# Weight products that alternate between two accumulator banks

## The chip, the cores and the metric

The kernel runs on one core of one Trainium2 chip. The metric is the device time of one execution in microseconds (us). Three runs of the kernel before gave 1007.35, 1008.02 and 1010.14 us; the median is 1008.02. The engines are TensorE (PE, with its weight loads PEld apart), VectorE (DVE), ScalarE (ACT), GpSimd (POOL) and SyncE (SP, which issues the DMAs).

## The reference

Two layers of a hybrid block on 256 tokens of width 1024, all in float32. Cut to what matters:

```python
def hybrid_layer(x, ...):
    h = _rms(x) * norm1_g
    proj = h @ w_in                       # 1024 -> 7680 columns
    aq, ak, av, rw, rq, rk, rv, rg, gates = _split(proj, IN_SIZES)
    o_a = sliding_window_attention(_rms(aq), _rms(ak), av, sinks) @ w_attn_o
    o_b = rwkv7_time_mix(rw, ...) @ w_rwkv_o       # recurrence over the tokens
    o_c = retention(rq, rk, rv, rg) @ w_ret_o      # rotary, chunks of 128, decay
    g = jax.nn.sigmoid(gates)
    mixed = g[0] * o_a + g[1] * o_b + g[2] * o_c
    x = x + mixed @ w_out
    h2 = _rms(x) * norm2_g
    return x + (jax.nn.silu(h2 @ w_ffn_gate) * (h2 @ w_ffn_up)) @ w_ffn_down   # 1024 -> 2816 -> 1024
```

Every matrix product with a weight (`w_in`, the three branch outputs, `w_out`, the three of the FFN) streams its weight once through the core.

## The kernel before, in words

**Splitting.** A float32 product is made of three products in a faster 32-bit format: each operand is split into a high part (rounded) and a low part (what is left), and high x high, high x low and low x high are added up in one accumulator.

**Weight stream.** `wunit` fetches 128 partitions x 1024 weights by one DMA (tile `raw`), casts them on ACT to the high part `wh`, and subtracts on DVE to get the low part `wl`. Each of the three tiles has three buffers. There are 292 such units in the program. A unit 512 columns wide holds two k-tiles (k-tile: 128 rows of the contraction).

**Token-major products.** The 256 tokens are two blocks of 128, t = 0 and 1. `gemm_tok` (around line 517 of the kernel before) computes, for both blocks, an accumulator of 128 tokens x 512 columns, one PSUM bank each. The activations are the stationary operand (128x128: one k-tile, one block), the weights stream past. For a unit it runs the first block through, k-tile by k-tile with three products each (`mm3`: high x `wh`, high x `wl`, low x `wh`), six products into the first bank; then six for the second block into the second. The names of the accumulators are those in the traces: `rq`, `rk`, `rv`, `rg` (retention), `aq`, `akv` (attention), `gt` (gates), `po` (branch outputs), `px` (output projection), `pfg`, `pfu` (FFN gate and up), `pd` (FFN down).

**Channel-major products.** The RWKV columns (`pf`, around line 690) have the weights stationary and the 256 tokens streaming, two channel blocks f = 0, 1 with an accumulator each, four k-tiles a unit, 24 products 256 wide: f = 0 first, then f = 1.

**From one product to the next.** A result that feeds another weight product is transposed on TensorE and split again, block by block: transposes into a side bank (`ptn` after a norm, `ptm` after the mixing, `pto` for the RWKV output, `ptf` in the FFN, `pta` for the attention queries), a cast on ACT (`hth`, `mth`, `obh`, `ath`: the high part) and a subtraction on DVE (`htl`, `mtl`, `obl`, `atl`: the low part). The residual `x` is updated by DVE straight from the accumulators `px` and `pd`; `xg` is `x` times the norm's weight.

**PSUM.** Four banks are for the accumulators of the weight products (two GEMMs of two banks each), four for everything else.

**Order.** Nothing runs in the order in which it is written. Class `Program` records every instruction, plans an order for all engines at once with a list schedule of its own costs, and emits it at one line (L399 in every profile row). The products of the weight streams keep the order in which they were recorded; everything else on TensorE goes between them when the planner holds it ready. Readers of an accumulator and the DMAs, casts and subtractions of the units have priority rules of their own (`key`). So another order of the products also moves instructions on ACT and DVE. The waits are set afterwards from what each instruction reads and writes.

Of the kernel before, what the change touches and what calls it, by code (L numbers as in the profile page):

```python
# [84 lines left out]
class _Engine:  # L85
    """An engine whose calls are recorded."""

# [20 lines left out]
class Program:  # L108
    """Records the instructions, orders them for the engines and emits them in that order.

    The order is a list schedule: products of the weight streams keep their order and form the backbone of TensorE,
    everything else goes in between by the length of what hangs on it. Tile sets the waits; nothing here does.
    stream: instructions of one stream take the buffers of a pool in their order
    unit:   number of the weight tile that an instruction prepares (split) or multiplies (bulk)
    urgent: ahead of all else on its engine (what frees an accumulator, the first loads)
    """

# [148 lines left out]
    def forward(self, succ, need, bl):  # L266
# [35 lines left out]
        def blocked(i):  # L302
            """the tag whose slot the op lacks, or None; est is raised to the slots' release"""
            for t in ops[i]["touch"]:
                if t in placed:
                    continue
                k, q = kq = self.tiles[t]
                if not free[k]:
                    return k
                lst = self.tags[k][1][q]  # L310
                while nxt[kq] < len(lst) and lst[nxt[kq]] in placed:
                    nxt[kq] += 1
                if lst[nxt[kq]] != t:
                    return k
                f, a = min(free[k])
                if a:
                    est[i] = max(est[i], f + self.lat(a, ops[i]["eng"], True))
            return None
# [88 lines left out]
def hybrid_kernel(ctx: ExitStack, tc: tile.TileContext, A: dict, cst_d: bass.AP, out: bass.AP, layers=L):  # L407
# [88 lines left out]

# [1 line left out]
    wcount = [-1]  # L498
# [13 lines left out]
    def mm3(ps, xh, xl, wh, wl, first, last):  # L512
        mm(ps, xh, wh, first, False)
        mm(ps, xh, wl, False, False)
        mm(ps, xl, wh, False, last)

    def gemm_tok(w, lhs, nkt, n, ps, kt0=0, tot=None, tts=(0, 1)):
        """ps[t] += lhs(kt)[:, t]^T w ; w is [nkt*128, n] of the k-range starting at kt0 of tot."""
        tot = nkt if tot is None else tot
        nk = 1024 // n  # L520
        for u in range(0, nkt, nk):
            c = min(nk, nkt - u)
            wh, wl = wunit(w[u * 128:(u + c) * 128, :], c, n)
            for t in tts:
                for k in range(c):
                    kt = kt0 + u + k
                    xh, xl = lhs(kt, t)
                    rec.bulk = True
                    mm3(ps[t][:, :n], xh, xl, wh[:, k, :], wl[:, k, :], kt == 0, kt == tot - 1)
                    rec.bulk = False  # L530

# [10 lines left out]
    def split(pt, hi, lo):  # L542
        """pt PSUM [128, n, 128] -> hi/lo slices."""
        S.copy(hi, pt)
        tt(lo, pt, hi.bitcast(F32), SUB)

# [1 line left out]
    def new_norm():  # L548
# [30 lines left out]

    # first norm  # L580
    st = new_norm()
# [6 lines left out]

    # per-channel vectors of both layers, channel on the partitions
    vraw = ST([68, 128], "vraw")  # L590
# [28 lines left out]
    for l in range(layers):  # L619
# [4 lines left out]

        # per-layer small operands
        wa2 = TL(lp, [128, 512], F32, tag="wa2", name="wa2")
# [9 lines left out]

        # ---- retention query first: it needs the first norm tiles only in order --
        def rope(ps, t):
# [30 lines left out]

# [1 line left out]
        dg = TL(z_p, [128, 2, 128], F32, tag="hs", name="dg")  # L671
# [16 lines left out]
        for u in (6, 2, 3, 0, 1, 4, 5):  # L688
            pf = [PG([128, T], "pf") for _ in range(2)]
            for kg in range(2):  # L690
                wh, wl = wunit(w_in[kg * 512:(kg + 1) * 512, 768 + 256 * u:768 + 256 * (u + 1)], 4, 256)
                hh, hl = hts[kg]
                for f in range(2):
                    for k in range(4):
                        a, b = wh[:, k, f * 128:(f + 1) * 128], wl[:, k, f * 128:(f + 1) * 128]
                        fst, lst = (kg == 0 and k == 0), (kg == 1 and k == 3)
                        rec.bulk = True
                        mm(pf[f], a, hh[:, k, :], fst, False)
                        mm(pf[f], a, hl[:, k, :], False, False)
                        mm(pf[f], b, hh[:, k, :], False, lst)  # L700
                        rec.bulk = False
            rec.stream = 1
# [8 lines left out]
            if u == 6:  # L711
                act(wa[0:64, :], wa[0:64, :], AF.Tanh)
                act(sg, sg, AF.Tanh, scale=0.5)
                ts(sg, sg, 0.5, 0.5, MUL, ADD)
                # decay and in-context rate
                tw = RT([128, 4, T], "tw")
# [30 lines left out]
        def head_sums(src, name):  # L747
            """sums over the channels of every head: [token, token block, channel block, head of it]"""
            ph = PS([128, T], name)
            for p in range(4):  # L750
                mm(ph[32 * p:32 * p + 32, :], C("hsel"), src[:, p, :])
            hsm = TL(z_p, [128, T], F32, tag="hsm", name="hsm", bufs=1)
            S.copy(hsm, ph)
            pt = PS([128, 2, 4, 32], name + "t")
            for t in range(2):
                P.transpose(pt[:, t].rearrange("p a b -> p (a b)"), hsm[:, t * 128:(t + 1) * 128], ident)
            return pt[:, :, :, 0:2]

        def rwkv_rest():
            vcol = lambda nm, p: vec[:, vo[nm] + l * 4 + p:vo[nm] + l * 4 + p + 1]  # L760
            # removal key, its head norm
            kq = RT([128, 4, T], "kq")
# [41 lines left out]

            # within-chunk products; rows are the source token of b (own half) and k (other half)
            GA = RT([128, 4, 4, 64], "GA")
# [17 lines left out]

            # inverse of the unit triangular matrices: 32-blocks with a problem per partition
            Y = RT([128, 32, 32], "Y")
# [33 lines left out]

            # values, token-major, and stacked under the state of each chunk
            vt = RT([128, 2, 512], "vt")
# [11 lines left out]
            for par in range(2):  # L874
                G.memset(SV[0][HR[par], 0, :, par, :], 0.0)
            # bonus sums
            rk = RT([128, 4, T], "rk")
# [5 lines left out]

            # chunk recurrence
            ysb = [RT([128, 8, 64], "ysb") for _ in range(2)]
# [45 lines left out]

            # group norm, bonus, gate
            lnx = MT([128, 2, 512], "lnx")
# [39 lines left out]

# [1 line left out]
        rec.stream = 3  # L975
        psq = proj_tok(0, 512, "aq")
        psk = proj_tok(512, 256, "akv")
        # high parts of a head's rows, its low parts on the other half of the partitions
        qs = [TL(m_p, [128, 2, 4, 128], F32R, tag="m", name="aqs") for _ in range(2)]
# [46 lines left out]
        for t in range(2):  # L1026
            nk = 128 * (t + 1)
            am = C("amask")[:, 256 - nk:256]
            # head order here is (g, kv): head = 4*kv + g
            sc = [MT([128, 4, nk], "sc") for _ in range(2)]  # L1030
# [24 lines left out]
            for kvh in range(2):  # L1055
                for g in range(4):
                    h = kvh * 4 + g
                    act(sc[kvh][:, g, :], sc[kvh][:, g, :], AF.Copy, scale=dn[:, h:h + 1])
                for kc in range(t + 1):
                    pt = PS([128, 4, 128], "ptp")  # L1060
                    for g in range(4):
                        P.transpose(pt[:, g, :], sc[kvh][:, g, kc * 128:(kc + 1) * 128], ident)
                    # store in the order (kv, parity of the head, half)
                    o4 = pT[kc].rearrange("p (k b i) q -> p k i b q", k=2, b=2)
                    S.copy(o4[:, kvh], pt.rearrange("p (i b) q -> p i b q", b=2))
# [9 lines left out]

# [1 line left out]
        rec.stream = 2  # L1077
# [62 lines left out]

# [1 line left out]
        rec.stream = 4  # L1142
# [42 lines left out]
        rec.stream = 0  # L1185
# [1 line left out]
        gbc = load_g(A["norm2_g"], l)  # L1187
# [14 lines left out]

# [1 line left out]
        hT2 = lhs_of(st["tiles"])  # L1204
# [66 lines left out]
```

## Time and profile before

| what | before |
|---|---|
| runs, median (lowest to highest) | 1008.02 us (1007.35 to 1010.14) |
| span of the profiled execution | 1008.4 us, 14757 instructions |
| TensorE busy | 987.7 us, 98% of the span, 5749 products and transposes |
| its loads | 810.6 us, 80% |
| DVE busy | 698.5 us, 69% |
| ACT busy | 506.4 us, 50% |
| mean granted TensorE clock | 0.990 |
| weights and other data moved | 161.12 MB, 160 GB/s |

The profiled execution's span is 1008.4 us, 0.4 above the median of the runs. A row of a timeline gives the start in us, the duration, the engine, the line, the operation, what it writes and reads without the tiles' numbers, and how often; in square brackets stands the idle time before it and what ended that. Products on TensorE are pipelined, so the distance from one start to the next is what a product costs, not the duration in its row. In the chain of work that ended last a row joins consecutive pieces of one kind: start, length, engine, tile, count.

### The profile page before, as it was taken

The page shows a single profiled execution, that of the slowest core. Times are in us where ns is not written, and L with a number is a line of the kernel's source. Part 1 is how long each engine was busy: PE and PEld are TensorE (multiplying, and loading weights), DVE is VectorE, ACT ScalarE, POOL GpSimd, SP SyncE. Part 2 cuts the span into 40 slices and gives each one's busy share as a digit, 9 for nine tenths or more (in the row PEclk, how much of TensorE's full clock was granted, in tenths as well). Part 3 has the DMA queues.
Part 4 walks back from the last instruction along what each step waited for, and adds up shares of the span by engine and source line. Part 5 has one row for each costly group of instructions (what it writes and reads, how often), then busy time and mean ns, then how long its engine had stood idle before and what let it go on. Part 6 is the DMA issues. An engine that isn't in the chain of part 4 may idle for free.

```text
span 1008.4 us, 14757 instructions
## 1 busy us (share of the span) xinstructions
PE 987.7 (98%) x5749; PEld 810.6 (80%) x5749; DVE 698.5 (69%) x1056; ACT 506.4 (50%) x757; POOL 41.2 (4%) x32
## 2 busy tenths in 40 slices
PE   6999999999999999999999999999999999999998
PEld 5988777877778888898878887778777888888886
DVE  5759998995787555554476699899857665555544
ACT  5735466445455544443367345573544464444432
POOL 0010100000200000000000110001002000000000
PEclk9989999999999999999999799999999999999999
DMA  7535543443356666655544344434523565666553
GB/s 256 180 107 172 163 126 105 134 158 106 106 200 181 205 186 182 190 183 188 188 154 138 105 148 147 146 112 139 169 84 125 193 185 177 191 189 186 178 187 126
DMA packets 94352, 161.12 MB, mean 160 GB/s; under 512 B 5894, under 2 KB 26570, under 8 KB 94282
## 3 DMA queue, kind: packets, MB, share of 16 engines
q1 hardware_dynamic: 94282, 160.18, 50.3%
q8 instruction: 45, 0.74, 0.3%
q14 instruction: 25, 0.20, 0.1%
HBM read 159.11 MB, written 1.05 MB: 159 GB/s over the span
## 4 chain that ended last, share of the span: by engine, by line
PE 83%; DVE 12%; issue 2%; DMA 1%; POOL 1%; ACT 1%; SPq 0%; DVEq 0%; POOLq 0%
PE pd L399 12%; PE pfg L399 12%; PE pfu L399 12%; PE gt L399 10%; PE pf L399 8%; PE po L399 7%; PE px L399 4%; DVE wl L399 4%; PE rg L399 2%; PE rq L399 2%; DVE X L399 1%; PE py L399 1%; DVE BK L399 1%; PE pas L399 1%; PE ptf L399 1%
## 5 line engine op out<-in xcount | busy, mean ns | idle before, releaser
L399 DVE TENSOR_TENSOR wl<-raw,wh 128x1024 fp32r<-128x1024 f32 x292 | 356.7, 1222 | 217.2 <-ACT wh L399 216.2
L399 ACT CAST wh<-raw 128x1024 fp32r<-128x1024 f32 x292 | 306.8, 1051 | 345.4 <-PE pd L399 68.4
L399 PE MATMUL gt<-wh,hth 128*128 128x512 f32 x192 | 77.9, 406 | 0.0
L399 PE MATMUL gt<-wh,htl 128*128 128x512 f32 x192 | 77.4, 403 | 0.0
L399 PE MATMUL gt<-wl,hth 128*128 128x512 f32 x192 | 76.6, 399 | 0.0
L399 PE MATMUL pfg<-wl,hth 128*128 128x512 f32 (+1 forms) x192 | 72.5, 377 | 0.0
L399 PE MATMUL pfg<-wh,htl 128*128 128x512 f32 (+1 forms) x192 | 72.3, 376 | 0.0
L399 PE MATMUL pfg<-wh,hth 128*128 128x512 f32 (+1 forms) x192 | 71.6, 373 | 0.0
L399 PE MATMUL pfu<-wh,hth 128*128 128x512 f32 (+1 forms) x192 | 71.3, 371 | 0.0
L399 PE MATMUL pfu<-wl,hth 128*128 128x512 f32 (+1 forms) x192 | 71.3, 371 | 0.0
L399 PE MATMUL pfu<-wh,htl 128*128 128x512 f32 (+1 forms) x192 | 71.3, 371 | 0.0
L399 PE MATMUL pd<-wh,atl 128*128 128x512 f32 x176 | 69.4, 394 | 0.0
L399 PE MATMUL pd<-wl,ath 128*128 128x512 f32 x176 | 69.3, 394 | 0.0
L399 PE MATMUL pd<-wh,ath 128*128 128x512 f32 x176 | 69.3, 393 | 0.0
L399 PE MATMUL pf<-hth,wh 128*128 128x256 f32 x224 | 68.0, 304 | 0.0
L399 PE MATMUL pf<-hth,wl 128*128 128x256 f32 x224 | 67.1, 300 | 0.1
L399 PE MATMUL pf<-htl,wh 128*128 128x256 f32 x224 | 66.7, 298 | 0.0
L399 PEld LDWEIGHTS pf<-hth,wh 128*128 128x128 f32 x224 | 45.8, 204 | 6.6 <-issue 6.5
L399 PEld LDWEIGHTS pf<-hth,wl 128*128 128x128 f32 x224 | 45.9, 205 | 1.9 <-issue 1.6
L399 PEld LDWEIGHTS pf<-htl,wh 128*128 128x128 f32 x224 | 45.9, 205 | 1.7 <-issue 1.6
L399 PEld LDWEIGHTS gt<-wl,hth 128*128 128x128 f32 x192 | 36.1, 188 | 8.3 <-DVE wl L399 0.6
L399 PEld LDWEIGHTS gt<-wh,hth 128*128 128x128 f32 x192 | 36.1, 188 | 7.8 <-issue 0.5
(312 smaller groups left out, 1936.2 us busy)
## 6 DMA issues: line engine op xcount, KB each, us to landing
raw<-in_w_in_dram SPq DMA_DIRECT2D x120, 512.0 KB, 3.6
raw<-in_w_ffn_gate_dram SPq DMA_DIRECT2D x44, 512.0 KB, 3.5
raw<-in_w_ffn_up_dram SPq DMA_DIRECT2D x44, 512.0 KB, 3.5
raw<-in_w_ffn_down_dram SPq DMA_DIRECT2D x44, 512.0 KB, 3.6
raw<-in_w_out_dram SPq DMA_DIRECT2D x16, 512.0 KB, 3.9
raw<-in_w_attn_o_dram SPq DMA_DIRECT2D x8, 512.0 KB, 3.8
raw<-in_w_ret_o_dram SPq DMA_DIRECT2D x8, 512.0 KB, 3.5
raw<-in_w_rwkv_o_dram SPq DMA_DIRECT2D x8, 512.0 KB, 3.5
```

The costliest lines, as they stand in the source:

```text
L399: o["fn"](*o["args"], **o["kw"])
```

## The change

The products of a unit are recorded in another order. In `gemm_tok`, for each k-tile, the two token blocks alternate product by product, and so do the two banks; the three products of a block are now high x `wh`, low x `wh`, high x `wl`, so `wl` comes last rather than second. In the RWKV loop the two channel blocks alternate in the same way, for each k-tile. Number, shape and operands of the products, the loads and the DMAs are the same; the instruction that closes an accumulator is now a product with `wl`. The rest of the difference is comments and blank lines.

```diff
     def gemm_tok(w, lhs, nkt, n, ps, kt0=0, tot=None, tts=(0, 1)):
...
             wh, wl = wunit(w[u * 128:(u + c) * 128, :], c, n)
-            for t in tts:
-                for k in range(c):
-                    kt = kt0 + u + k
-                    xh, xl = lhs(kt, t)
-                    rec.bulk = True
-                    mm3(ps[t][:, :n], xh, xl, wh[:, k, :], wl[:, k, :], kt == 0, kt == tot - 1)
-                    rec.bulk = False
+            rec.bulk = True
+            for k in range(c):
+                kt = kt0 + u + k
+                xs = [lhs(kt, t) for t in tts]
+                fst, lst = kt == 0, kt == tot - 1
+                for i, t in enumerate(tts):
+                    mm(ps[t][:, :n], xs[i][0], wh[:, k, :], fst, False)
+                for i, t in enumerate(tts):
+                    mm(ps[t][:, :n], xs[i][1], wh[:, k, :], False, False)
+                for i, t in enumerate(tts):
+                    mm(ps[t][:, :n], xs[i][0], wl[:, k, :], False, lst)
+            rec.bulk = False
...
                 hh, hl = hts[kg]
-                for f in range(2):
-                    for k in range(4):
-                        a, b = wh[:, k, f * 128:(f + 1) * 128], wl[:, k, f * 128:(f + 1) * 128]
-                        fst, lst = (kg == 0 and k == 0), (kg == 1 and k == 3)
-                        rec.bulk = True
-                        mm(pf[f], a, hh[:, k, :], fst, False)
-                        mm(pf[f], a, hl[:, k, :], False, False)
-                        mm(pf[f], b, hh[:, k, :], False, lst)
-                        rec.bulk = False
+                rec.bulk = True
+                for k in range(4):
+                    fst, lst = (kg == 0 and k == 0), (kg == 1 and k == 3)
+                    for w, x, a, z in ((wh, hh, fst, False), (wh, hl, False, False), (wl, hh, False, lst)):
+                        for f in range(2):
+                            mm(pf[f], w[:, k, f * 128:(f + 1) * 128], x[:, k, :], a, z)
+                rec.bulk = False
```

What the planner makes of it is shown at three places. First TensorE at the border from the output projection to the FFN in layer one: the first products of `pfg_709` (t = 0) and `pfg_710` (t = 1), before:

```order
L399 MATMUL pfg_709<-wh_712,hth_683 128x512
L399 MATMUL pfg_709<-wl_713,hth_683 128x512
L399 MATMUL pfg_709<-wh_712,htl_684 128x512
L399 MATMUL pfg_709<-wh_712,hth_683 128x512
L399 MATMUL pfg_709<-wl_713,hth_683 128x512
L399 MATMUL pfg_709<-wh_712,htl_684 128x512
L399 MATMUL pfg_710<-wh_712,hth_683 128x512
L399 MATMUL pfg_710<-wl_713,hth_683 128x512
L399 MATMUL pfg_710<-wh_712,htl_684 128x512
```

Now, the same place:

```order
L399 MATMUL pfg_709<-wh_712,hth_683 128x512
L399 MATMUL pfg_710<-wh_712,hth_683 128x512
L399 MATMUL pfg_709<-wh_712,htl_684 128x512
L399 MATMUL pfg_710<-wh_712,htl_684 128x512
L399 MATMUL pfg_709<-wl_713,hth_683 128x512
L399 MATMUL pfg_710<-wl_713,hth_683 128x512
```

The first product with `htl` for the second block was the ninth and is the fourth. On DVE its last part, `htl_684<-ptn_689`, stands behind both updates of `x` from `px` in both orders.

Second, ACT at the border from the gates to the RWKV branch's output product (`po_635`, `po_636`): casts of the transposed RWKV output (`obh_337`, from the transposes `pto_345` for t = 0 and `pto_352` for t = 1), gate activations `tg` and casts of weight units, before:

```order
L399 CAST obh_337<-pto_345 128x4x128
L399 ACTIVATE tg_633<-gt_619,nhrs_126 128x512
L399 CAST obh_337<-pto_352 128x4x128
L399 ACTIVATE tg_634<-gt_620,nhrs_126 128x512
L399 CAST wh_650<-raw_649 128x1024
```

Now:

```order
L399 CAST obh_337<-pto_345 128x4x128
L399 CAST wh_650<-raw_649 128x1024
L399 ACTIVATE tg_633<-gt_619,nhrs_126 128x512
L399 ACTIVATE tg_634<-gt_620,nhrs_126 128x512
L399 CAST obh_337<-pto_352 128x4x128
```

The second cast of `obh` went behind a weight cast and both activations. On TensorE the transposes `pto_352` moved from the middle of the last gate unit to its end, right ahead of the first `po` product:

```order
L399 MATMUL gt_619<-wl_632,hth_116 128x512
L399 MATMUL gt_620<-wl_632,hth_116 128x512
L399 MATMUL pto_352<-cst_105,ysb_304 128x128 x4
L399 MATMUL po_635<-wh_638,obh_337 128x512
L399 MATMUL po_636<-wh_638,obh_337 128x512
L399 MATMUL po_635<-wh_638,obl_338 128x512
L399 MATMUL po_636<-wh_638,obl_338 128x512
```

Before, five products of `gt_620` came after `pto_352`, and then six of `po_635`; the first product of `po_636` was the seventh and is now the second.

Third, TensorE in the retention value product (`rv`), where the attention queries are transposed (`pta`), before:

```order
L399 MATMUL rv_454<-wl_463,hth_116 128x512
L399 MATMUL rv_454<-wh_462,htl_117 128x512
L399 MATMUL rv_454<-wh_462,hth_116 128x512
L399 MATMUL pta_386<-cst_105,qn_385 128x128 x4
L399 MATMUL ptk_387<-cst_105,kv_380 128x128
L399 MATMUL pta_395<-cst_105,qn_394 128x128 x4
L399 MATMUL ptk_396<-cst_105,kv_389 128x128
L399 MATMUL rv_454<-wl_463,hth_116 128x512
```

Now:

```order
L399 MATMUL rv_453<-wh_459,htl_109 128x512
L399 MATMUL rv_454<-wh_459,htl_109 128x512
L399 MATMUL rv_453<-wl_460,hth_108 128x512
L399 MATMUL pta_386<-cst_105,qn_385 128x128 x4
L399 MATMUL ptk_387<-cst_105,kv_380 128x128
L399 MATMUL pta_395<-cst_105,qn_394 128x128 x4
L399 MATMUL ptk_396<-cst_105,kv_389 128x128
L399 MATMUL rv_454<-wl_460,hth_108 128x512
```

`pta` moved up by one unit less one product: eleven products. On DVE the tile `GR`, whose operations free the side banks that `pta` takes, moved ahead of one weight subtraction (`wl_466`).

## The prediction

> **What bounds the kernel now.** I read the page first (busy shares, granted clock, chain that ended last), then TensorE's list of waits, then timelines of TensorE, VectorE (DVE) and ScalarE (ACT) wherever a product of a weight stream waits or nearly waits.
>
> ```profile
> PE 987.7 (98%) x5749; PEld 810.6 (80%) x5749; DVE 698.5 (69%) x1056; ACT 506.4 (50%) x757; POOL 41.2 (4%) x32
> ...
> PEclk9989999999999999999999799999999999999999
> ...
> PE 83%; DVE 12%; issue 2%; DMA 1%; POOL 1%; ACT 1%; SPq 0%; DVEq 0%; POOLq 0%
> ```
>
> TensorE is busy for 98% of the span at a clock of nine tenths or more, and the chain that ended last is mostly TensorE. So two things can move the time: the spacing of the products, and the places where TensorE stands still. The second are few (total us, times, longest):
>
> ```profile
> PE ptn L399 <- DVE xg L399: 6.7, 2, 6.5
> PE pta L399 <- DVE GR L399: 2.0, 2, 1.0
> PE pz L399 <- DVE Tn L399: 1.9, 2, 1.1
> PE pss L399 <- ACT kq L399: 1.2, 1, 1.2
> ...
> PE pto L399 <- DVE ysb L399: 1.1, 2, 0.6
> ```
>
> Apart from 6.7 us at the start they come to some 7 us. The spacing stands in the chain in order of time, and product by product in TensorE's timeline:
>
> ```profile
> 330.94 10.88 PE pfu L399 x48
> ```
> ```profile
> 376.14 0.39 PE L399 MATMUL pfu<-wh,hth 128*128 128x512 f32 x1
> ...
> 377.27 0.39 PE L399 MATMUL pfu<-wh,htl 128*128 128x512 f32 x1
> 377.50 0.39 PE L399 MATMUL pfu<-wh,hth 128*128 128x512 f32 x1
> 377.72 0.39 PE L399 MATMUL pfu<-wl,hth 128*128 128x512 f32 x1
> ```
>
> 10.88 us over 48 is 226.7 ns a product. 376.14 is the first pfu product of a unit, so 377.27 (five steps on) is the sixth and 377.50 the first into the other bank: 0.23 across the switch, 0.22 behind it.
>
> **Spacing: 0.** The change removes no product and no load. It makes a bank switch of every step where it was one in six, and the switch above costs what any other step costs. 3024 of the 3984 weight products are 512 wide, so 1 ns each would be 3 us. The one stage with another spacing is the down projection:
>
> ```profile
> 446.29 58.73 PE pd L399 x254
> ```
>
> That is 231.2 ns, 4.5 more than pfu; over its 528 products 2.4 us, and about as much again in po. [...] I take 0, with bounds of -4 (the excess gone) and +4 (doubled).
>
> **What moves: when the second token block's low part is needed.** Within a unit of two k-tiles the first block had six products before the second began, so the second block's low part was read by the ninth product. Now it is read by the fourth: five products, 5 x 0.227 = 1.13 us, earlier. And the two accumulators of a GEMM now end one product apart, so the first one's reader on DVE starts five products later than it could. Where one GEMM feeds the next, both squeeze the same DVE queue. I price each border by its rows.
>
> *px to pfg (output projection to FFN), each layer:*
>
> ```profile
> 319.31 0.39 PE L399 MATMUL pfg<-wh,hth 128*128 128x512 f32 x1
> ...
> 320.45 0.40 PE L399 MATMUL pfg<-wh,htl 128*128 128x512 f32 x1
> ```
> ```profile
> 318.35 1.28 DVE L399 SCALAR_TENSOR_TENSOR x<-px,x 128x512 f32<-128x512 f32 x2
> 319.55 0.68 DVE L399 TENSOR_TENSOR htl<-ptn,hth 128x512 fp32r<-128x512 f32 x1
> ...
> 1004.64 0.69 DVE L399 TENSOR_TENSOR x<-pd,x 128x512 f32<-128x512 f32 x1 [0.69 <-PE pd L399]
> ```
> ```profile
> 1004.21 0.39 PE L399 MATMUL pd<-wh,atl 128*128 128x512 f32 x1
> ```
>
> Before, htl was ready at 320.23 and read at 320.45. A reader that waits for an accumulator starts 0.43 us after its last product (1004.21 to 1004.64). 319.31 is pfg's fourth product, so px's last two stand four and five steps ahead of it, at 318.40 and 318.18. Now they close one bank each, so the reads begin at 318.61 instead of 318.35, and htl, behind both, is ready at 320.49. The fourth product would start at 319.31: a wait of 1.2 us, 2.4 for two layers. Below: 0.5 each, if ACT and DVE reach the reads idle and htl's transposes land between them.
>
> *po to px, each layer:*
>
> ```profile
> 295.46 0.39 PE L399 MATMUL px<-wh,mth 128*128 128x512 f32 x1
> ...
> 296.62 0.39 PE L399 MATMUL px<-wh,mtl 128*128 128x512 f32 x1
> ```
> ```profile
> 294.40 1.28 DVE L399 SCALAR_TENSOR_TENSOR tg<-tg,po 128x512 f32<-128x512 f32 x2
> 295.60 0.68 DVE L399 TENSOR_TENSOR mtl<-ptm,mth 128x512 fp32r<-128x512 f32 x1
> ```
>
> The same: 295.46 is px's fourth product, po's last but one, which now closes the first bank, stands five steps ahead of it at 294.30, its read at 294.73 instead of 294.40, mtl ready near 296.6, the fourth product due at 295.46: 1.15 each, 2.3 together (0.5 to 1.3 each).
>
> *gt to po of the RWKV branch, each layer.* Here the planner also moved four transposes (pto) from the middle of the last gate unit to its end, just ahead of po, and on ACT put a weight cast and two gate activations ahead of the cast obh that follows them.
>
> ```profile
> 281.19 0.69 ACT L399 ACTIVATE tg<-gt,nhrs 128x512 f32<-128x512 f32 x1 [0.34 <-PE gt L399]
> 281.86 0.59 ACT L399 CAST obh<-pto 128x512 fp32r<-128x512 f32 x1
> ...
> 283.61 1.04 ACT L399 CAST wh<-raw 128x1024 fp32r<-128x1024 f32 x1
> ```
> ```profile
> 281.97 1.28 DVE L399 TENSOR_TENSOR obl<-pto,obh 128x512 fp32r<-128x512 f32 x2
> ```
> ```profile
> 282.82 0.40 PE L399 MATMUL po<-wh,obh 128*128 128x512 f32 x1
> ```
>
> Before, both obl were done at 283.25. Now the cast that goes ahead needs the buffer of the last gate unit, free near 282.0; with 1.04 for it, twice 0.65 for the activations and 0.6 for obh, obh's second half is there at 284.9, obl's at 285.6. po's second product, the first of block 1, was due at 283.05: it waits 1.85, the fourth 0.2 more. I take 2.0 each, 4.0 together. Below: 0.8, if the ACT queue were empty (transposes end near 283.2, plus 0.6 for the cast). Above: 2.2.
>
> *pd to rq, the layer border, once:*
>
> ```profile
> 509.36 0.50 PE L399 MATMUL rq<-wh,htl 128*128 128x512 f32 x1 [1.14 <-DVE htl L399]
> ...
> 514.48 0.67 PE L399 MATMUL prb<-dg,cst 128*128 128x256 f32 x2 [0.83 <-DVE nhrs L399]
> ```
>
> By the new DVE order prb can start at 513.4, but with 10 products of rq behind it, not 17: 7 x 0.227 - 1.05 = +0.5 (0 to 1.5).
>
> *The end:* the two last additions come after both banks close, so the second runs behind the first: 0.43 + 0.6 after the product ahead of the last, +0.4.
>
> **Gains and the middle of a layer.**
>
> ```profile
> 10.69 0.68 DVE L399 TENSOR_TENSOR htl<-ptn,hth 128x512 fp32r<-128x512 f32 x1
> ```
> ```profile
> 10.83 0.80 PE L399 MATMUL rq<-wl,hth 128*128 128x512 f32 x1 [0.46 <-DVE wl L399]
> ...
> 11.85 0.63 PE L399 MATMUL rq<-wh,hth 128*128 128x512 f32 x1
> ```
>
> At the start the second product no longer needs wl, and the fourth can go when htl is there (11.4) instead of at 11.85: -0.25 (-0.43 to 0).
>
> ```profile
> 118.82 1.23 DVE L399 TENSOR_TENSOR wl<-raw,wh 128x1024 fp32r<-128x1024 f32 x1
> ```
> ```profile
> 120.64 0.63 PE L399 MATMUL pta<-cst,qn 128*128 128x128 f32 x4 [0.99 <-DVE GR L399]
> ```
>
> The attention transposes pta stand 11 products (2.5 us) earlier in TensorE's order, while only one weight subtraction (1.23) went behind GR on DVE: they wait 1.27 longer. DVE, though, is nearly full through this stretch:
>
> ```profile
> 100.00:125.00 25.00, 23.75 (x126) 19.64 (x126) 24.44 (x45) 11.42 (x19) 3.42 (x2) 1.00 0.53 162
> ```
>
> (window and its length, then the busy time of TensorE, its loads, DVE, ACT and GpSimd). It has the same work in the end, and pz, back at its old place but one product, waits 1.05 for it in the old order. A TensorE that is 1.27 late finds pz's operand there: 0.3 a layer, 0.6 together (each from -1.05, wait gone and nothing lost, to +1.3, nothing absorbed). The wait of pss in layer two falls by most of its 1.2, since about 12 narrow products now stand ahead of it: -0.9. pto's waits lose half: -0.6, the recurrence ahead of them having moved up three products. Last, the new order goes twelve times more from weight products to transposes and back. In the chain four transposes take, to what follows them,
>
> ```profile
> 121.38 0.44 PE pta L399 x4
> ...
> 128.58 0.59 PE ptb L399 x4
> ```
>
> so the place is worth at most 0.15: twelve by 0 to 0.15; at 0.05 each, since 0.44 is the commoner row, +0.6.
>
> **Sum:** -0.25 + 2.4 + 2.3 + 4.0 + 0.5 + 0.4 + 0.6 - 0.9 - 0.6 + 0.6 = +9.05 us on a profiled span of 1008.4, so 1017.4. The runs' median of 1008.02 lies 0.4 under that span; I forecast 1017.
>
> **Rivals.**
>
> *Faster: banks set the spacing.* If writing one bank back to back cost something, alternation would take it off every product. At 0.22, the smallest step in the rows above, it is 6.7 ns x 3024 = 20 us, less the 9 of the stalls: 997. It decides from 3 ns a product on. Against it: the switch row. [...]
>
> *No change: the queues give it back.* DVE's waits behind ACT are short and TensorE's six waits above shrink by whatever it is late. If px, po and pd lose half of their terms (4.8 instead of 9.6 with the end), pta and pz together give 2.1, pss and pto 2.3, and the excess in pd falls away (2.4), the span is 1008.4 + 4.8 - 6.8 = 1006.4, and with the excess kept 1008.8. For it: those waits exist. Against: the large terms stand at borders where TensorE waits for nothing today, so nothing is there to shrink.
>
> *Slower still: the middle isn't absorbed.* If pta's 1.3 stays and the softmax transposes, moved up by 22 products, lose up to 1.5 as well, each layer loses 2.5 more: 1022.4. It decides if DVE loses time to TensorE between 120 and 226 us.
>
> *The clock.* A step of rq in the first, cold microseconds is 0.43 (11.85, with 11.42 the product ahead of it), not 0.227. If alternation made the clock drop for a tenth of the span, the work of that tenth would take nearly twice as long: some 90 us more, 1098. The clock row shows nothing of the kind at today's switches. [...] Here no idle is seen at a switch.
>
> That the change does not take place can be left out: in the new order every pair of products alternates.
>
> **Chances.** Forecast (1011 to 1021) 0.62; not absorbed 0.13; no change 0.16; faster by spacing 0.06; clock 0.03. A measurement of this kernel tells about 0.3%, 3 us, from no change. Slower: 0.62 + 0.13 + 0.03 less a little of the forecast's low edge = 0.77. Same: 0.15. Faster: 0.06 and a third of what no change has below 1005 = 0.08. The range of 8 in 10 is 1009 to 1024: spacing bounds and the border terms' low ends below, the unabsorbed case above. The forecast's own range is 1011 to 1021.
>
> **What would show it.** Right: dense pfu still 10.9 us for 48; new entries in TensorE's waits of about 1.2 us for htl at pfg and mtl at px, about 2 us for obh and obl at po, twice each; pz's and pss's waits smaller; the end 0.4 later. Wrong: a changed pfu spacing (rival one), a clock row with low digits, border waits under 0.5, or pta's longer wait without a shorter one at pz.

## The result, and the profile after

The changed kernel took 1023.32 us (median of four runs, 1021.24 to 1025.01) against 1008.9 us for the kernel before (now the median of four): a ratio of 1.0134, 95% interval 1.0109 to 1.0160. It is slower by 14.4 us. I forecast slower, 1017, with 1009 to 1024 as the range: the direction held, the size was too small by 6 us, and it came partly from other places than I had said. That the time still lies inside the range, 0.7 us under its top, is luck in part, as the stretches below show.

The page of the changed kernel, busy times and granted clock:

```profile
PE 993.9 (97%) x5749; PEld 809.4 (79%) x5749; DVE 700.1 (68%) x1056; ACT 501.5 (49%) x757; POOL 38.6 (4%) x32
...
PEclk9999999999999999999999799999999999999999
```

The work is the same, and so is the mean clock (0.991, before 0.990); the span is 1023.2 instead of 1008.4. The dense stretches did not change either. TensorE's timeline in the FFN (pairs of products into the two banks):

```profile
340.03 0.62 PE L399 MATMUL pfu<-wl,hth 128*128 128x512 f32 x2
340.48 0.62 PE L399 MATMUL pfu<-wh,hth 128*128 128x512 f32 x2
340.94 0.61 PE L399 MATMUL pfu<-wh,htl 128*128 128x512 f32 x2
341.39 0.62 PE L399 MATMUL pfu<-wl,hth 128*128 128x512 f32 x2
```

1.36 us over six products is 227 ns, a bank switch at every step. So the loss is in waits. TensorE's list (total, times, longest) leads, behind the 5.9 us at the start, with four lines that the list before did not have:

```profile
PE po L399 <- ACT obh L399: 3.3, 2, 1.6
PE rk L399 <- ACT kv L399: 2.2, 2, 1.2
PE pfg L399 <- DVE htl L399: 2.1, 2, 1.1
PE px L399 <- DVE mtl L399: 2.1, 2, 1.1
PE pz L399 <- DVE Tn L399: 1.6, 2, 0.9
PE pta L399 <- DVE GR L399: 1.6, 2, 0.8
...
PE pto L399 <- DVE ysb L399: 0.7, 1, 0.7
PE pss L399 <- ACT kq L399: 0.7, 1, 0.7
```

Both kernels run the same products of the weight streams, unit by unit. So the start of a unit's first product in the changed kernel, less that in the kernel before, says how late the change has made the program by then (taken where both have as many transposes and other small products behind them). Its steps are where the time went:

| stretch | layer one | layer two | I had said, both layers |
|---|---|---|---|
| start (layer one) | -0.4 | | -0.25 |
| the border pd to rq | | +0.5 | +0.5 |
| rq and the RWKV columns (pf) | -2.3 | -0.8 | -0.9 |
| to the end of rk | +2.0 | +2.0 | nothing |
| rv, attention, first branch output | +2.2 | +2.2 | +0.6 with pz |
| to the last gate unit | -0.5 | -0.5 | nothing |
| gt to po (RWKV branch) | +3.9 | +1.4 | +4.0, and -0.6 for pto |
| po to px | +1.1 | +1.1 | +2.3 |
| px to pfg | +1.0 | +1.0 | +2.4 |
| rest of the FFN | +0.1 | +0.4 | 0 (spacing, -4 to +4) |
| the last additions | | +0.5 | +0.4 |

Apart from rounding they add up to 14.8, the difference of the two spans (the column of what I had said leaves out the 0.6 for changes between products and transposes, which has no stretch of its own). Each figure compares one execution with one execution, and the first rows depend on which: f1, g1 and g2 below have the changed kernel's order on TensorE, ACT and DVE well beyond the columns of layer one, and they reached the first product of aq 0.7 late, 2.9 early and 0.4 late; the changed kernel was 2.7 early. So neither the start's -0.4 nor the columns' -2.3 can be put down to the order.

**The two low-part borders** went as the prediction's working had it, here px to pfg in layer one, TensorE and then DVE:

```profile
325.06 0.39 PE L399 MATMUL pfg<-wh,htl 128*128 128x512 f32 x1
326.52 0.50 PE L399 MATMUL pfg<-wh,htl 128*128 128x512 f32 x1 [1.07 <-DVE htl L399]
```
```profile
324.58 1.29 DVE L399 SCALAR_TENSOR_TENSOR x<-px,x 128x512 f32<-128x512 f32 x2 [0.62 <-PE px L399]
325.79 0.68 DVE L399 TENSOR_TENSOR htl<-ptn,hth 128x512 fp32r<-128x512 f32 x1
```

DVE now waits for px to close (0.62), reads both banks, and only then makes the htl that the fourth product needs; 1.07 of TensorE's time passes.

**gt to po**, TensorE and ACT, layer one:

```profile
283.88 0.47 PE L399 MATMUL po<-wh,obh 128*128 128x512 f32 x1
286.00 0.50 PE L399 MATMUL po<-wh,obh 128*128 128x512 f32 x1 [1.64 <-ACT obh L399]
```
```profile
283.26 1.05 ACT L399 CAST wh<-raw 128x1024 fp32r<-128x1024 f32 x1 [1.26 <-PE gt L399]
284.21 1.26 ACT L399 ACTIVATE tg<-gt,nhrs 128x512 f32<-128x512 f32 x2
285.36 0.58 ACT L399 CAST obh<-pto 128x512 fp32r<-128x512 f32 x1
```

The queue on ACT is the one worked out: weight cast, two activations, then obh, and po's second product waits 1.64 for it.

**rk**, which I had not seen. TensorE and ACT, layer one:

```profile
94.58 0.39 PE L399 MATMUL rk<-wh,hth 128*128 128x512 f32 x1
96.16 0.50 PE L399 MATMUL rk<-wh,hth 128*128 128x512 f32 x1 [1.19 <-ACT kv L399]
```
```profile
94.69 1.05 ACT L399 CAST wh<-raw 128x1024 fp32r<-128x1024 f32 x1 [1.86 <-PE akv L399]
95.64 0.83 ACT L399 ACTIVATE kv<-akv,nrs 128x256 f32<-128x256 f32 x2
```

It is the second product of rk that waits, the first into its second bank, and what it waits for is not an operand: kv is the reading of akv, which frees a bank. In the old order the second bank was opened by the seventh product, and akv's first bank was closed and read while its second was still being filled. TensorE and ACT before, the first and the seventh product of rk and the two readings of akv:

```profile
97.29 0.40 PE L399 MATMUL rk<-wh,hth 128*128 128x512 f32 x1
...
98.68 0.39 PE L399 MATMUL rk<-wh,hth 128*128 128x512 f32 x1
```
```profile
96.05 0.47 ACT L399 ACTIVATE kv<-akv,nrs 128x256 f32<-128x256 f32 x1 [0.17 <-PE akv L399]
...
97.49 0.47 ACT L399 ACTIVATE kv<-akv,nrs 128x256 f32<-128x256 f32 x1 [0.62 <-PE akv L399]
```

One bank was read out at 96.52, before rk began, the other at 97.96, before rk's seventh product.

### The profile page after: what moved, and what is told of

It is laid out like the page before. It is cut to its first block, busy times and chain, and to the rows that moved or that the text cites. A ratio compares the mean times of both kernels' runs of the same rounds, so it can differ in the third digit from the quotient of the medians.

```text
span 1023.2 us, 14767 instructions
## 1 busy us (share of the span) xinstructions
PE 993.9 (97%) x5749; PEld 809.4 (79%) x5749; DVE 700.1 (68%) x1056; ACT 501.5 (49%) x757; POOL 38.6 (4%) x32
## 5 line engine op out<-in xcount | busy, mean ns | idle before, releaser
L399 PE MATMUL gt<-wh,hth 128*128 128x512 f32 x192 | 63.0, 402 | 0.0
L399 PE MATMUL pfg<-wh,htl 128*128 128x512 f32 (+1 forms) x192 | 57.0, 375 | 2.1 <-DVE htl L399 2.1
L399 PE MATMUL pfu<-wh,hth 128*128 128x512 f32 (+1 forms) x192 | 55.7, 371 | 0.0
L399 PE MATMUL pfu<-wl,hth 128*128 128x512 f32 (+1 forms) x192 | 55.7, 371 | 0.0
L399 PE MATMUL pfu<-wh,htl 128*128 128x512 f32 (+1 forms) x192 | 55.7, 371 | 0.0
L399 PE MATMUL pf<-htl,wh 128*128 128x256 f32 x224 | 49.5, 298 | 0.0
L399 PE MATMUL pf<-hth,wh 128*128 128x256 f32 x224 | 48.0, 297 | 0.0
L399 PE MATMUL pf<-hth,wl 128*128 128x256 f32 x224 | 47.4, 294 | 0.0
L399 PEld LDWEIGHTS gt<-wh,htl 128*128 128x128 f32 x192 | 35.3, 188 | 8.9 <-issue 1.2
L399 PEld LDWEIGHTS pfg<-wh,htl 128*128 128x128 f32 x192 | 35.0, 188 | 9.1 <-DVE htl L399 3.0
```

The source lines that it names most:

```text
L399: o["fn"](*o["args"], **o["kw"])
```

## Experiments

The theory after this reading: alternation is free in a dense stream; it costs at a few units where a GEMM meets the one ahead of it, because (a) the second block's operand is needed five products earlier, (b) two banks are opened at once and closed at once. The rival: something in alternating, or in the order of the three products, costs everywhere. Every ratio below is to the kernel before, measured in the same set of runs.

### Where in the stream it costs

**e1_pf_only**: only the RWKV loop alternates.

```diff
-            (gemm_tok as changed)
+            for t in tts:
+                for k in range(c):
+                    mm3(ps[t][:, :n], xh, xl, wh[:, k, :], wl[:, k, :], kt == 0, kt == tot - 1)
```

> Only the channel-major RWKV loop (pf) alternates between its two banks; every gemm_tok product is in the old order. Border theory (the loss comes from token block 1's low part being needed by the fourth instead of the ninth product, and from both accumulators of a token-major GEMM closing together): pf has no such border, its operands are ready for both channel blocks, so 1006 to 1011, no change. Rival (each alternating product costs something, about 14.4 us over 3984 products): pf is 960 narrow products, so +1.7 to +3.5 us, 1011 to 1012.

1009.49 us, ratio 0.9995 (0.9982 to 1.0007). No change: 672 alternating products cost nothing (pf has 672; the 960 of the expectation are all the narrow ones, and for 672 its rival gives at most 2.4 us).

**e2_inner_only** and **e3_edges_only** divide gemm_tok's units; pf is in the old order in both. The counts in the expectations are of the 126 units a layer that are 512 wide; six narrower ones are all edges.

```diff
+            if kt0 + u == 0 or kt0 + u + c == tot:    # e2: old order here; e3: old order elsewhere
+                (first block, then second, mm3)
+            else:
                 (alternating)
```

> gemm_tok alternates in every unit except the first and the last of a GEMM's contraction, which keep the old order; pf keeps the old order. That is 64 of 126 units a layer. Border theory: neither border is touched, 1007 to 1012, and no waits of pfg for htl, px for mtl or po for obh. Rival, a cost per alternating product: half of the loss, 1015 to 1017.

> The opposite: only the first and the last unit of a GEMM's contraction alternate, 62 of 126 units a layer; the units between and pf keep the old order. Border theory: nearly the whole loss, 1018 to 1024, with the waits of pfg for htl (1.0 each), px for mtl (1.1 each) and po for obh (1.6 each) as in the changed kernel. Rival, a cost per alternating product: half of the loss, 1015 to 1017, and half of these waits would be unexplained.

e2: 1009.22, ratio 0.9989 (0.9975 to 1.0003). e3: 1024.32, ratio 1.0134 (1.0119 to 1.0149). Half of the alternating units carry none of the loss, the other half as much as the whole change. A cost per product is out, and so is a cost of the bank switch. But e3's loss is not the changed kernel's, place by place: by the same reckoning as in the table it loses 8.3 us (layer one) and 3.7 (layer two) between the first product of rk and the first branch output, where the changed kernel loses 4.2 in each, and 1.0 and 0.6 from there to the first product of px, where the changed kernel loses 3.4 and 0.9. That the totals are equal is partly chance.

e3's waits have px and rk, as the changed kernel has, but none of pfg for htl and none of po for obh (which I had expected):

```profile
PE px L399 <- DVE mtl L399: 2.1, 2, 1.0
PE rk L399 <- ACT kv L399: 2.1, 2, 1.0
```

Its pfg did alternate at the border. In its order htl stands ahead of both reads of px on DVE (at 328.43 us, they at 329.03); so alternation at a border need not wait, and it depends on the neighbours that the planner gives it.

**e4_wl_last**: no alternation, only the new order of the three products.

```diff
-                    mm3(...)                                    # xh wh, xh wl, xl wh
+                    mm(ps, xh, wh, first, False)
+                    mm(ps, xl, wh, False, False)
+                    mm(ps, xh, wl, False, last)
```

> No alternation at all: in gemm_tok one token block is finished before the other, as before, but the three products are in the new order (high x wh, low x wh, high x wl). pf as before. Border theory: the second block's low part is needed by the eighth instead of the ninth product, 0.23 us earlier with a slack of 0.2 to 0.3 before, so at most 0.1 to 0.3 at each border, and the start gains 0.4 because wl is needed one product later: 1007 to 1011. Rival (the order of the three products makes the loss, not the alternation): 1018 to 1024.

1018.48, ratio 1.0087 (1.0061 to 1.0113): a miss. Nothing at the borders (px and pfg lose 0.1 to 0.2 each), but the planner laid out the middle otherwise; the longest wait of pz doubled (before: 1.9 in all, 1.1 the longest):

```profile
PE pz L399 <- DVE Tn L399: 3.0, 2, 2.1
```

So whatever moves the products' needs by a step makes another plan of the whole program, and another plan of the middle can be 9 us worse without any border; which of its moves costs what was not taken apart. So part of the change's loss could be the price of a new plan rather than of alternation; e1 and e2 have new plans too, and lose nothing. This makes single sums like the prediction's uncertain, and it is why the next experiments change single units of the changed kernel, with most of its plan kept.

### The borders

**f1_borders_old** puts back into the old order, in the changed kernel, the last gate unit, the first and last unit of the RWKV output product, the first and last of px, the first of pfg, the last of pd and the first rq of layer two. **f2_borders_only** is the reverse. (That is seven units in layer one and eight in layer two; the expectations, which say nine, miscounted.)

```diff
+        gemm_tok(..., edge="f" / "l" / "")     # the units named above
+            if not (("f" in edge and u == 0) or ("l" in edge and u + c == nkt)):   # f1; f2 without the not
                 (alternating)
+            else:
+                (first block, then second, mm3)
```

> The changed kernel, with nine units a layer put back into the old order: the last gate unit, the first unit of the RWKV output product, its last unit, the first and last of the output projection, the first of the FFN gate, the last of the down projection, and in layer two the first of the retention query. All else alternates, pf too. Border theory (by the changed kernel's trace: px 1.1 and pfg 1.0 a layer, po 3.5 and 1.4, the end 0.3): 1012 to 1015, without the waits of px for mtl, pfg for htl and po for obh; what is left over the kernel before comes from the middle of the layers. Rival (the three products' order or the planner's middle carry the loss everywhere): 1019 to 1023.

> The kernel before, with only those nine units a layer in the new order. Border theory: the waits of px 1.1, pfg 1.0 and po 1.5 to 3.5 a layer come back although 117 of 126 units are as before: 1016 to 1019. Rival (the middle of the layers carries the loss): 1008 to 1011.

f1: 1014.62, ratio 1.0044 (1.0028 to 1.0061). The waits of px, pfg and po are gone, and 8.7 us with them; rk's stays (2.3), and the middle of its layers loses what the changed kernel's does. As expected. f2: 1014.15, ratio 1.0040 (1.0024 to 1.0056): 4 us, less than I had expected, and the loss lies at gt to po alone (2.6 in layer one, 4.2 in layer two, less small gains elsewhere). The wait of po came back,

```profile
PE po L399 <- ACT obh L399: 4.2, 2, 2.1
```

those of px and pfg did not. DVE's timeline of f2 at px to pfg shows why:

```profile
320.69 0.68 DVE L399 TENSOR_TENSOR htl<-ptn,hth 128x512 fp32r<-128x512 f32 x1
321.29 1.28 DVE L399 SCALAR_TENSOR_TENSOR x<-px,x 128x512 f32<-128x512 f32 x2
```

The same products on TensorE as in the changed kernel at this place, but htl ahead of the reads: no wait.

**g1_low_part_ahead** tests this queue in the changed kernel itself.

```diff
-    def split(pt, hi, lo):
+    def split(pt, hi, lo, ahead=False):
+        was, rec.urgent = rec.urgent, rec.urgent or ahead     # ahead: column block 0 of ptn and ptm
         S.copy(hi, pt)
         tt(lo, pt, hi.bitcast(F32), SUB)
+        rec.urgent = was
```

> The changed kernel, all alternating; only the planner's priority of the cast and the subtraction that make mtl and htl ahead of the two borders is raised, so that on DVE the second half of mtl (htl) stands between the two reads of the accumulators po (px), not behind both. If the border wait is that queue on DVE, each of the four waits loses one read, 0.6 us, and stays at 0.4 to 0.5: 2.4 us together, 1020 to 1022. Rival (alternation itself, whatever stands on DVE): waits of 1.0 to 1.1 as before, 1023.

1019.85, ratio 1.0099 (1.0079 to 1.0120), 3.5 us under the changed kernel's median. DVE at px to pfg, and the two waits:

```profile
323.84 0.69 DVE L399 SCALAR_TENSOR_TENSOR x<-px,x 128x512 f32<-128x512 f32 x1 [0.62 <-PE px L399]
324.45 0.68 DVE L399 TENSOR_TENSOR htl<-ptn,hth 128x512 fp32r<-128x512 f32 x1
325.05 0.68 DVE L399 SCALAR_TENSOR_TENSOR x<-px,x 128x512 f32<-128x512 f32 x1
```
```profile
PE pfg L399 <- DVE htl L399: 1.0, 2, 0.5
PE px L399 <- DVE mtl L399: 0.9, 2, 0.5
```

htl passed one of the two reads, and each of the four waits lost one read, 0.6, as expected. The border wait is that queue. The rest of the 3.5 us is not: the edit raises the same parts behind every norm, and at the border pd to rq, where the changed kernel loses 0.5, this one wins 0.3.

### The bank

**g2_rk_first_old**: the changed kernel, with one unit a layer in the old order.

```diff
+            gemm_tok(w_in[:, c0:c0 + n], hT, 8, n, ps, old=name == "rk")
+            if not (old and u == 0):
                 (alternating)
```

> The changed kernel, with one unit in the old order: the first of the retention key GEMM (rk), so that its second accumulator bank is opened by the seventh product, not by the second. If the wait of rk for kv (1.2 and 1.0) is the missing bank, which kv frees only when akv's two accumulators have closed together, it is gone or under 0.2 in both layers, and each layer is 1 to 2 us shorter at the end of rk: 1019 to 1022. Rival (rk waits for something that the order of its own products doesn't touch): the wait stays, 1023.

1016.11, ratio 1.0063 (1.0038 to 1.0089): 7.2 us less than the changed kernel for one unit in each layer. Its wait list, and TensorE where rk's second bank opens:

```profile
PE rk L399 <- ACT kv L399: 0.2, 1, 0.2
```
```profile
99.41 0.50 PE L399 MATMUL rk<-wh,hth 128*128 128x512 f32 x1 [0.21 <-ACT kv L399]
```

The wait is the bank. The gain is larger than the 2.2 us of the wait: the next stretch, from rv to the first branch output, which lost 2.2 a layer, now loses 0.2. The plan behind rk is another one as well (pg's waits for aqs, 1.0 in all, are gone), so how much of the second 2.2 comes from the late rk and how much from the new plan stays open. f1 and g2 change different units of the same kernel and win 8.7 and 7.2 us, together somewhat more than the 14.4 that the change cost; a kernel with both was not run.

**f5_w_in_only**: only the token-major products with w_in alternate.

```diff
-            gemm_tok(w_in[:, c0:c0 + n], hT, 8, n, ps)
+            gemm_tok(w_in[:, c0:c0 + n], hT, 8, n, ps, alt=True)      # all other calls: old order
```

> Only the token-major products with w_in alternate (attention, retention and gate projections); the branch outputs, the output projection, the FFN and pf keep the old order. If the middle of the layer loses by itself (3.5 us a layer by the changed kernel's trace, at rk and between rv and the attention products): 1014 to 1017, with the wait of rk for kv near 1.0 a layer. If the borders are all: 1008 to 1011.

1019.85, ratio 1.0089 (1.0058 to 1.0119), above my 1014 to 1017: the middle alone makes two thirds of the loss, with rk's 2.1 in its list and no line for px, pfg or po. With f2's 0.4% it gives 1.3%, the whole, but that is no proof: f1's 0.4% and f2's 0.4% should give the whole as well and give 0.8%, and f2 lost nothing at px and pfg. Parts of a plan do not simply add.

### The order of the three products, with alternation

**f3_alt_old_products**: block 1's low part is needed by the sixth product.

```diff
-                for i, t in enumerate(tts): mm(..., xs[i][1], wh ...)     # low x wh second
-                for i, t in enumerate(tts): mm(..., xs[i][0], wl ...)
+                for i, t in enumerate(tts): mm(..., xs[i][0], wl ...)     # as before: wl second
+                for i, t in enumerate(tts): mm(..., xs[i][1], wh ...)
```

> gemm_tok alternates product by product, but the three products of a block stay in the old order (high x wh, high x wl, low x wh); pf as in the changed kernel. The second block's low part is then needed by the sixth product, not the fourth, two products or 0.45 us later. Border theory: px's and pfg's waits 0.5 to 0.7 each in place of 1.1 and 1.0, the wait of po for the second half of obh still there unless the casts on ACT come in another order; with the middle as in the changed kernel 1016 to 1020. Rival (the order of the three products is the loss, since it alone cost 0.9%): 1007 to 1011.

1018.58, ratio 1.0074 (1.0048 to 1.0101), within the range, for another reason than I gave: its list has no wait of px, pfg or po at all, and rk's is 0.4. Its profiled execution loses 10 us in one place, between rv and the first branch output of layer one, where the clock is at half (TensorE, loads, DVE, ACT and GpSimd busy, then the clock):

```profile
132.00:136.00 4.00, 4.00 (x14) 2.83 (x13) 2.70 (x6) 2.27 (x7) 0.95 (x1) 0.50 0.38 99
136.00:140.00 4.00, 4.00 (x13) 3.35 (x14) 2.09 (x4) 2.44 (x14) 0.00 (x0) 0.50 0.08 32
```

The mean clock of that whole execution is 0.989. The runs of f3 spread from 1014.1 to 1021.7. What lowered the clock there was not found.

### Looking for a better version

e2 is the best alternating kernel and does not differ from the kernel before. All kernels up to here run part of the RWKV columns at half clock in their profiled executions (3.4 to 10.2 us a layer, not the 8 to 10 of the expectation below; 10.2 in both layers of the kernel before, 3.4 and 10.2 in the changed one), where small products (pb) stand between few narrow ones. The same window, before and after the change:

```profile
62.00:78.00 16.00, 16.00 (x80) 12.23 (x79) 9.05 (x18) 3.59 (x7) 0.00 (x0) 0.68 0.21 63
```
```profile
62.00:78.00 16.00, 16.00 (x104) 13.27 (x103) 10.58 (x20) 4.59 (x8) 0.00 (x0) 0.89 0.33 99
```

The difference, 16 us x 0.21 = 3.4 us of work, covers the changed kernel's gain of 2.3 in layer one, but it varies: f1 and g2, with the same order up to there, have 0.79 in this window, and g1 0.89. Two kernels put more narrow products between them by the planner's bound on TensorE's use, on e2's order.

```diff
-TAU, UCOLD, UWARM, UMIN = 2000, 0.45, 0.75, 0.6
+TAU, UCOLD, UWARM, UMIN = 2000, 0.45, 0.75, 0.7      # h2: 0.8
```

> The kernel that alternates only in the inner units, with the planner's lower bound on TensorE's use raised from 0.6 to 0.7: five instead of three narrow products stand between pairs of the small pb products. The granted clock falls to 0.5 there for about 8 to 10 us a layer in every kernel so far. If that stretch of sparse work is the cause, the clock holds longer: 2 to 6 us less, 1003 to 1007. If not: 1008 to 1010.

> The same with the bound at 0.8: eight narrow products between pairs of pb. If the sparse stretch is the cause, the clock stays at full speed in both layers: 3 to 8 us less, 1001 to 1006, unless the later pb costs more in the stretch behind it. If not: 1008 to 1012.

h1: ratio 1.0060 (1.0036 to 1.0083), median 1016.22 of five; four runs lay between 1010.4 and 1018.8 and one took 1620.5. The clock did hold in its profiled execution, the shortest (mean 0.999; 0.990 to 0.994 in the other three of the four),

```profile
66.00:70.00 4.00, 4.00 (x22) 2.45 (x22) 1.25 (x2) 1.05 (x1) 0.00 (x0) 1.00 0.30 113
```

and 2.4 us were ahead at the end of layer two's columns, but the stretches behind gave them back: span 1008.6. h2: 1048.83, ratio 1.0389 (1.0358 to 1.0421). In its profiled execution (mean clock 0.985) 17 us of layer one's columns ran at half clock. pto waits 5.7 us in all for ysb, the recurrence's output, where it waited 1.1 before, so the later pb seems to make the recurrence late; where the rest of the 40 us goes was not taken apart. Both are misses; no kernel here beats the one before.

## Why the prediction was right or wrong

**Spacing 0: right.** 227 ns at every switch, and e2 with 0.9989, where half of the wide units alternate. The rivals that lived on it, faster by spacing and the clock, are out: no product came faster, and the clock row above is as flat as before, its mean 0.991 against 0.990. The bounds of -4 and +4 were the author's estimate from the larger step of pd (231.2 ns before); no run shows what sets that step. In the changed kernel 46 steps of pd from 454.02 us on took 10.70 us, 232.6 ns each, so it neither fell to pfu's nor doubled its excess.

**The two low-part borders: right in mechanism and near in size.** 1.2 and 1.15 were forecast, 1.0 and 1.1 measured, and g1 took exactly the read away that the working had put ahead of htl. What the working lacked is that this is the planner's DVE order and no property of the border: in f2 the same products wait for nothing, and in e3 pfg does not wait (px does, 1.0 each).

**gt to po: right in mechanism, mis-sized.** 2.0 a layer forecast, 3.9 and 1.4 measured for a wait of 1.64 in both. 1.4 us of the difference is the clock: after the wait in layer one it fell, and seven steps of po took 0.427 us each, not 0.227; in layer two it did not fall after the same wait. Two windows of 2 us, behind the first wait and behind the second:

```profile
288.00:290.00 2.00, 2.00 (x6) 1.57 (x5) 0.00 (x0) 0.45 (x1) 0.00 (x0) 0.50 0.37 142
...
794.00:796.00 2.00, 2.00 (x11) 1.61 (x10) 0.00 (x0) 0.56 (x1) 0.00 (x0) 1.00 0.67 238
```

Another 0.7 is pto, which waited that long in layer one and not at all in layer two; 0.4 is left.

**The middle: wrong, and here the missing time lies** (8.4 us in both layers where I had 0.6; what came out better elsewhere hides a part of it). The step that failed is the one on pta and pz: 0.3 a layer, since DVE is nearly full there and pz would absorb what pta loses. I had looked for queues only where one GEMM feeds the next. pta did not wait longer (1.6 in all, 2.0 before), because TensorE reached it late: rk had waited. In g2, where rk hardly waits, pta waits 1.3 each, more than before but not the 2.3 worked out, and the stretch loses 0.2 a layer, near the 0.3; there the plan behind rk is another, though. The operand was the only thing I followed; the accumulator banks are the other thing that alternation needs earlier and frees later (rk waited 1.19 for one; in g2 0.2). That the two accumulators end one product apart stood in the prediction, but only for their readers on DVE, not for the GEMM that takes the bank next. The middle lost 2.0 and 2.2 a layer where I had 0.3, and its rival, "not absorbed", gave 1022.4, close to what came, for a reason that was not the one: that closeness is luck, and so is a part of the range's holding, since its top was set by this rival.

**Small terms.** Start -0.4 (forecast -0.25) and end +0.5 (forecast +0.4):

```profile
1018.72 1.29 DVE L399 TENSOR_TENSOR x<-pd,x 128x512 f32<-128x512 f32 x2 [1.49 <-PE pd L399]
```

both additions run one behind the other after the banks close. The border pd to rq lost 0.5, exactly as worked out: ten products of rq stand ahead of prb, not 17, and prb starts at 520.48 after a wait of 0.83. Less the 7.05 that the program was late by the last unit of pd, that is the 513.4 of the prediction. pss lost 0.7 where 1.2 was: a gain of 0.5, not 0.9. pto lost 0.7 where 1.1 was: a gain of 0.4, not 0.6. The columns gained 2.3 in layer one, which no step had; as said above, executions with the same order do not all show it, nor the start's gain.

## What to carry to other kernels

Switching accumulator banks from product to product cost this dense stream nothing (227 ns a product as before), but it changes when things are needed: the second block's operand half a unit earlier, the second bank at once, and both banks' readers together at the end. Before interleaving two accumulations, look at the first and the last unit of each GEMM: who makes the second operand, behind what in its engine's queue, and who frees the bank. Alternate inside, finish one accumulator first at the edges (e2: ratio 0.9989); and where a planner makes the order, read its new order at those places, since here a neighbour in a queue decided whether the border waited (pfg for htl: 1.07 in the changed kernel, no wait in e3).

## What the runs showed of the hardware that was not expected

The clock fell after a wait of less than 2 us in one place and not in another: behind a wait of 1.64 us for obh it went to 0.50 for some 3 us in layer one (clock 0.86, 0.50 and 0.79 in three windows of 2 us) and stayed at 1.00 in layer two of the same execution. In f2, with a wait of 2.1 in each layer, it fell in layer two, where gt to po lost 4.2 against 2.6 in layer one:

```profile
786.00:788.00 2.00, 2.00 (x6) 1.55 (x5) 0.00 (x0) 0.16 (x1) 0.00 (x0) 0.50 0.54 189
```

What decides stays open. TensorE stood still for 1.64 us in the changed kernel and for 2.1 us in f2; in layer one of the changed kernel it had also waited 0.74 us for pto, up to 279.88. In the columns there was no wait at all: in the window from 62 to 78 us of the kernel before TensorE is busy for all 16 us, part of it with pb products of 8 rows, and the mean clock is 0.68.
